# One 512-column product for two token streams in a feed-forward's up projection

## The chip, the cores and the metric

The kernel runs on one core of a Trainium2 chip. The metric is the device time of one execution in microseconds (us), the median over several runs. The core's engines are named as in the profile: PE (TensorE, matmuls), PEld (TensorE's weight loads, which overlap PE), DVE (VectorE), ACT (ScalarE), POOL (GpSimd) and SP (SyncE, which here issues the large loads).

## The reference, cut to what matters

Two small transformer models run one behind the other on 256 tokens x of width 1024. In the first model's first layer a second stream of 256 context tokens, ctx, goes through the same layer with the same weights and its own modulation, so its feed-forward takes both streams; D_FF is 2816.

```python
def modulate(h, shift, scale):
    return h * (1 + scale) + shift

def conv_ffn(h, w_up, conv_w, conv_b, w_down):
    a = h @ w_up
    a = lax.conv_general_dilated(a, conv_w, window_strides=(1,), padding=((CONV_W // 2, CONV_W // 2),),
                                 dimension_numbers=('NWC', 'WIO', 'NWC'),
                                 feature_group_count=a.shape[-1]) + conv_b
    gate, val = jnp.split(a, 2, axis=-1)
    return (jax.nn.silu(gate) * val) @ w_down

# first_block, layer i
x = x + g2 * conv_ffn(modulate(rms_norm(x, norm2_g[i]), sh2, sc2),
                      w_up[i], conv_w[i], conv_b[i], w_down[i])
if not last:
    ...
    ctx = ctx + cg2 * conv_ffn(modulate(rms_norm(ctx, norm2_g[i]), csh2, csc2),
                               w_up[i], conv_w[i], conv_b[i], w_down[i])
```

## The kernel before, in words

All is float32, and each operand of a large product is split into a high part and a low rest (wh and wl of the weights, hH and hL of the normed and modulated tokens h, gH and gL of the gated values). A product is then the sum of three matmuls, high by high (L285), high by low (L286) and low by high (L289), written once in `mms`: for each half of the inner tiles k, and in it for each output bank b, the first two kinds alternate over k, and the third follows for both banks. The weights are the stationary operand (a 128x128 tile), the tokens the moving one.

The first feed-forward, `ffn(0)` with T = 512, has 22 chunks `up` (128 gate and 128 value columns each, two PSUM banks of a tile S, of which there are two) in six groups of 4, 4, 4, 4, 3 and 3, and behind each group its `down` products, 8 tiles of 128 outputs with 512 tokens as moving columns (acc). Behind the first up of a group stands the down of the group before. Between them, as filler, are the products of a modulation (L410, weights wm loaded at L366). An up works through stream 0 (x, h in the tiles hH and hL of pool `hp`) and then through stream 1 (ctx, h in the tiles hcH and hcL of the pool of 8 KB buffers, x8), 256 moving columns each: 2 streams x 2 banks x 8 k x 3 matmuls = 96. Then ACT and DVE evacuate S with the convolution (L988, L991, L993), silu (L1021), product (L1024) and split (L1028, L1029).

Weights come as two halves w by DMA from SP (L224), are cast to wh by ACT (L238) in pieces of 384, 384 and 256 columns, and DVE subtracts to get wl (L240). Of the pairs wh, wl two stand in a pool of their own, wp; in the plan of loads every third pair takes two buffers of x8 (`wtile`). In the first feed-forward these are the pairs of up chunks 2, 6, 10, 14, 18 and 21, and of the two pairs of a down (outputs 0 to 3, outputs 4 to 7) the first, in the first four groups.

The norm in front of it, `h_split` and `h_tile`, makes h tile by tile: DVE scales (ht, L529), ACT adds the shift and rounds (L539), DVE takes the rest (L540); for some tiles of stream 0 ACT and POOL do that (L535 to L537).

PE and SP run in a written order: a planner (`Line`) interleaves the pieces of work, and each `yield` of `mms` tells it the time of a half, reckoned from columns. ACT, DVE and POOL are put in order by an automatic scheduler, which works with its own estimates of when things are ready.

Of the kernel before, what the change touches and what calls it, by code (L numbers as in the profile page):

```python
# [12 lines left out]
F32R = mybir.dt.float32r  # L13
# [6 lines left out]
P = 128  # L20
D = 1024
NT = 256
KD = D // P
# [3 lines left out]
CH = 2048  # L27
# [5 lines left out]
class Line:  # L33
# [4 lines left out]
    def __init__(self):  # L38
        self.now, self.pend, self.live = 0.0, [], {}
# [40 lines left out]
def spread(main, fill):  # L80

    out, done = [], 0
    for i, u in enumerate(main):
        out.append(u)
        want = len(fill) * (i + 1) // len(main)
        out += fill[done:want]
        done = want
    return out + fill[done:]

# [7 lines left out]
WHOLE = ()  # L99
# [6 lines left out]
class Stack:  # L106
# [406 lines left out]
            nc.tensor.matmul(ps, lhsT=self.ones, rhs=sq, start=ft == 0, stop=ft == KD - 1)  # L513
        return {"ps": ps}

    def h_room(self, s, whole=False):
        if whole:
            t = self.hp.tile([P, CH], F32, tag="hH", name="h") if s == 0 else self.x8("hc")
            self.h[s] = (t.rearrange("p (k t) -> p k t", k=KD),)
        elif s == 0:  # L520
            self.h[s] = tuple(self.hp.tile([P, KD, NT], F32R, tag=t, name=t) for t in ("hH", "hL"))
        else:
            self.h[s] = tuple(self.x8(t, F32R).rearrange("p (k t) -> p k t", k=KD) for t in ("hcH", "hcL"))
# [18 lines left out]
    def h_split(self, i, j, g, r, s, pre=None, pool=(), wait=0):  # L542


        A = self.mod_scale(i, j + 1, g, s)
        B = self.mods(i, j)
        self.h_room(s, (i, j) == (1, 0) and "win1" in WHOLE)
        for ft in range(KD):
            if pre is not None:
                pre(ft)  # L550
            self.h_tile(ft, A[:, ft:ft + 1], B[:, ft, s:s + 1], r, s, ft in pool)
            if wait and ft < KD - 1:
                yield 0, wait
# [152 lines left out]
    def block1(self, l, after):  # L706
# [233 lines left out]
        seq += heavy[:n]  # L940
        seq += need("c00", "c01", *(f"c{c}{s}" for c in (1, 2) for s in streams))
        seq += spread(bs(range(4)), spread(heavy[n:], fill[0]))
        seq += need(*(f"c{c}{s}" for c in (3, 4, 5) for s in streams), "c31", "c51")
        bnames = [f"b{p}{s}1" for p in range(4) for s in streams]
        cc = cs_()
        if l == 1:
            seq += [lambda: self.go(self.ctx2_norm(), "cx")]
        w0 = wouts(0, slice(0, T))
        seq += cc[:2] + need(*bnames) + spread(cc[2:], spread(w0, fill[1]))
        seq += need(*(f"g{s}" for s in streams))  # L950
        seq += need("c_0011", "c_1011")
        for a, b in MOVES[l]:
            seq.insert((a + b) % len(seq), seq.pop(a % len(seq)))
        if l == 1:
            seq = seq[:12] + spread(seq[12:], self.more_units((1, 12, 20)))
# [40 lines left out]
    def ffn(self, i, T, streams, after):  # L996


        nc, key = self.nc, f"sm{i}"
        post = i >= 2  # L1000
        groups = FF_GROUPS[T]
        starts = [sum(groups[:g]) for g in range(len(groups))]
        nst = {q: {} for q in streams}
        y = self.x8("y").rearrange("p (k t) -> p k t", k=KD) if post else None
        gt = {}
        cols = 512 if T == 512 else 256

        def up(g, j):
            a = j - starts[g]
            if a == 0:  # L1010
                gt[g] = tuple(self.gp.tile([P, groups[g], T], F32R, tag=t, name=t) for t in ("gH", "gL"))
            wh, wl = self.weights(f"wup{i}", j, k=KD)
            ps = self.psum("S", [P, 2, 512])
            for q in streams:
                hH, hL = self.h[q]
                yield from self.mms([ps[:, b, 256 * q:256 * q + 256] for b in range(2)], range(KD),
                         lambda b, k: (wh[:, k, P * b:P * b + P], wl[:, k, P * b:P * b + P]),
                         lambda b, k: (hH[:, k], hL[:, k]))
            c = self.pt.tile([P, 2, 512], F32, tag="pt", name="cgv")
            self.conv(c[:, 0, :T], ps[:, 0, :T], key, j)  # L1020
            nc.scalar.activation(c[:, 0, :T], c[:, 0, :T], AF.Silu)  # L1021
            if i < 2:
                self.conv(c[:, 1, :T], ps[:, 1, :T], key, KF + j)
                nc.vector.tensor_tensor(c[:, 1, :T], c[:, 0, :T], c[:, 1, :T], ALU.mult)  # L1024
            else:
                nc.vector.tensor_tensor(c[:, 1, :T], c[:, 0, :T], ps[:, 1, :T], ALU.mult)
            gH, gL = gt[g]
            nc.scalar.copy(gH[:, a], c[:, 1, :T])  # L1028
            (nc.vector if T == 512 else nc.gpsimd).tensor_tensor(gL[:, a], c[:, 1, :T], gH[:, a].bitcast(F32), ALU.subtract)  # L1029
            if j == KF - 1:  # L1030
                self.lnexp()

        def down(g, ft, c):
            gk = groups[g]
            cc, f4 = divmod(ft, cols // P)
            wh, wl = self.weights(f"wdn{i}", g, cc, k=gk)
            gH, gL = gt[g]
            fs = slice(P * f4, P * f4 + P)
            acc = self.psum("acc", [P, 512])
            yield from self.mms([acc[:, c]], range(gk), lambda b, k: (wh[:, k, fs], wl[:, k, fs]),  # L1040
                     lambda b, k: (gH[:, k, c], gL[:, k, c]))
            last = g == len(groups) - 1
            if not post:
                self.residual(i, 5, acc, ft, [q for q in streams if c.start <= 256 * q < c.stop])
                if last:
                    self.sumsq(nst[c.start // 256], self.xs[c.start // 256][:, ft], ft == KD - 1)
            else:
                if g == 0:
                    nc.scalar.copy(y[:, ft], acc[:, :256])
                else:  # L1050
                    nc.vector.tensor_tensor(y[:, ft], y[:, ft], acc[:, :256], ALU.add)
                if last:
                    self.post_sums(nst[0], y[:, ft], ft, i == 3)

        main = []
        for kind, g, j in self.ffn_order(T):
            if kind == "up":
                main.append(lambda g=g, j=j: self.go(up(g, j)))
            elif g < len(groups) - 1:
                main += [lambda g=g, ft=ft: self.go(down(g, ft, slice(0, T))) for ft in range(KD)]  # L1060
        for u in spread(main, self.fill_f(i)):
            u()
        if i == 0:
            self.prep1(1)
        if post:
            nst[0] = self.post_start(i, 5, self.sm(key, "post2"))
        for q in streams:
            for ft in range(KD):
                self.go(down(len(groups) - 1, ft, slice(256 * q, 256 * q + 256)))
                if i == 2:  # L1070
                    self.early_loads(ft)
            after(q, nst[q], y)
# [553 lines left out]
```

## Time and profile before

| | us |
|---|---|
| median of 3 runs | 1751.69 |
| lowest, highest | 1749.96, 1760.24 |
| the profiled execution's own time | 1754.48 |
| its span, first to last instruction | 1752.7 |

The profiled execution is 2.79 us above the median, and 1.8 us of its time lie outside the span. Its mean granted TensorE clock is 0.967 of full speed. The first feed-forward takes the stretch from about 312 to 716 us. A row with an operation and a number ("PE S L289 x8") gives what was written (S) and the line; the profile cuts a matmul's busy time so that in the chain of waits each piece lasts from one start to the next, while a mean in the groups counts the overlap of pipelined matmuls twice.

### The profile page before, as it was taken

Reading aid. Unit: us, or ns where it says so; the run is one execution under the profiler, and the core shown is the slowest. Engines: PE = TensorE matmul, PEld = TensorE weight load, DVE = VectorE, ACT = ScalarE, POOL = GpSimd, SP = SyncE. Lnnn points to the kernel's source line nnn. Section 1 sums busy time; section 2 is a strip of 40 time slices with the busy share of each in tenths; the row PEclk is TensorE's granted clock in tenths of the full one; section 3 lists DMA queues with packets and bytes.
Section 4 is the critical chain, followed back from the end, with each engine's and each line's share of the span. In section 5 each row is a group of like instructions: output and inputs, shape, how many; then the busy total and the mean of one; then the engine's idle time right before and its main releaser. Section 6 shows DMA issues by size and latency. Waiting matters only on the chain.

```text
span 1752.7 us, 32334 instructions
## 1 busy us (share of the span) xinstructions
PE 1599.5 (91%) x12604; PEld 1419.1 (81%) x12604; DVE 1188.5 (68%) x2877; ACT 879.1 (50%) x2147; POOL 136.7 (8%) x162
## 2 busy tenths in 40 slices
PE   6999797999999999889888998988979999779997
PEld 5877457989898989788468998976869999479996
DVE  5765886755555545777788777785776567876665
ACT  6344654523242324455546656563556555656563
POOL 1000001000000000010000101000141012330110
PEclk9999998999999999999899999999989999889999
DMA  8344330444545454334334544565554546435552
GB/s 326 107 145 145 125 125 32 146 182 177 219 143 217 168 205 176 131 119 154 133 109 151 195 167 139 175 220 208 197 180 164 196 155 226 174 118 196 170 176 88
DMA packets 67402, 288.36 MB, mean 165 GB/s; under 512 B 7728, under 2 KB 9008, under 8 KB 54960
## 3 DMA queue, kind: packets, MB, share of 16 engines
q1 hardware_dynamic: 65664, 283.91, 46.0%
q10 hardware_dynamic: 1584, 2.38, 0.4%
q8 instruction: 99, 1.62, 0.4%
q14 instruction: 55, 0.45, 0.1%
HBM read 285.21 MB, written 1.05 MB: 163 GB/s over the span
## 4 chain that ended last, share of the span: by engine, by line
PE 61%; DVE 18%; DMA 10%; ACT 7%; issue 3%; POOL 1%; SPq 0%; ACTq 0%; DVEq 0%; POOLq 0%
PE S L285 9%; PE S L286 9%; PE S L289 9%; PE acc L285 8%; PE acc L286 8%; PE acc L289 8%; DVE wl L240 6%; DMA w<-in_wup_dram 5%; PE acc L410 3%; ACT wh L238 2%; DMA w<-in_wdn_dram 2%; DVE ht L529 1%; PE tr L671 1%; DMA wm<-in_wmod_dram 1%; DVE mx L661 1%
## 5 line engine op out<-in xcount | busy, mean ns | idle before, releaser
L240 DVE TENSOR_TENSOR wl<-w,wh 128x384 fp32r<-128x384 f32 (+2 forms) x1010 | 489.1, 523 | 218.5 <-ACT wh L238 190.7
L238 ACT CAST wh<-w 128x384 fp32r<-128x384 f32 (+2 forms) x1010 | 421.3, 475 | 329.4 <-DMA w<-in_wup_dram 94.9
L285 PE MATMUL S<-hH,wh 128*128 128x256 f32 x1408 | 351.3, 287 | 31.0 <-ACT hH L539 17.4
L286 PE MATMUL S<-hL,wh 128*128 128x256 f32 x1408 | 349.2, 285 | 4.7 <-POOL hL L537 4.0
L285 PEld LDWEIGHTS S<-hH,wh 128*128 128x128 f32 x1408 | 271.6, 193 | 36.9 <-ACT hH L539 18.1
L286 PEld LDWEIGHTS S<-hL,wh 128*128 128x128 f32 x1408 | 271.5, 193 | 7.1 <-POOL hL L537 5.0
L285 PE MATMUL acc<-gH,wh 128*128 128x256 f32 (+1 forms) x728 | 209.0, 311 | 9.2 <-DVE xc L980 4.8
L286 PE MATMUL acc<-gL,wh 128*128 128x256 f32 (+1 forms) x728 | 205.3, 306 | 0.0
L289 PE MATMUL S<-hH,wl 128*128 128x256 f32 x1408 | 198.4, 284 | 0.0
L289 PEld LDWEIGHTS S<-hH,wl 128*128 128x128 f32 x1408 | 182.6, 193 | 0.0
L285 PEld LDWEIGHTS acc<-gH,wh 128*128 128x128 f32 x728 | 138.9, 191 | 23.6 <-issue 7.0
L289 PE MATMUL acc<-gH,wl 128*128 128x256 f32 (+1 forms) x728 | 145.7, 306 | 0.0
L286 PEld LDWEIGHTS acc<-gL,wh 128*128 128x128 f32 x728 | 138.9, 191 | 5.5
L991 DVE SCALAR_TENSOR_TENSOR cgv<-S,sm,cgv 128x255 f32<-128x255 f32 (+1 forms) x132 | 74.8, 567 | 67.6 <-ACT cgv L988 67.1
L289 PEld LDWEIGHTS acc<-gH,wl 128*128 128x128 f32 x728 | 110.2, 191 | 6.5
L988 ACT ACTIVATE cgv<-S,sm 128x256 f32<-128x256 f32 (+1 forms) x132 | 82.7, 628 | 47.3 <-PE S L289 47.3
L285 PE MATMUL acc<-wh,hH 128*128 128x256 f32 x344 | 91.2, 296 | 10.4 <-ACT hH L539 8.2
L1029 POOL TENSOR_TENSOR gL<-cgv,gH 128x256 fp32r<-128x256 f32 x66 | 52.2, 791 | 579.5 <-ACT gH L1028 558.7
L980 DVE SCALAR_TENSOR_TENSOR x<-acc,mod,x 128x256 f32<-128x256 f32 x104 | 50.0, 482 | 57.7 <-PE acc L289 57.3
L286 PE MATMUL acc<-wl,hH 128*128 128x256 f32 x344 | 88.1, 287 | 0.0
L286 PE MATMUL S<-hcL,wh 128*128 128x256 f32 x352 | 86.5, 284 | 0.3 <-DVE hcL L540 0.3
L285 PE MATMUL S<-hcH,wh 128*128 128x256 f32 x352 | 86.4, 280 | 0.0
(268 smaller groups left out, 2837.4 us busy)
## 6 DMA issues: line engine op xcount, KB each, us to landing
wm<-in_wmod_dram SPq DMA_DIRECT2D x72, 1024.0 KB, 7.6
w<-in_wup_dram SPq DMA_DIRECT2D x140, 512.0 KB, 3.9
w<-in_wdn_dram SPq DMA_DIRECT2D x56, 512.0 KB, 4.1
mw<-in_wmod_dram SPq DMA_DIRECT2D x48, 512.0 KB, 4.7
w<-in_wup_dram SPq DMA_DIRECT2D x18, 1024.0 KB, 7.5
w<-in_win_dram SPq DMA_DIRECT2D x32, 512.0 KB, 4.0
w<-in_wout_dram SPq DMA_DIRECT2D x16, 512.0 KB, 4.7
w<-in_wqkv_dram SPq DMA_DIRECT2D x16, 512.0 KB, 3.9
```

The source lines that it names most:

```text
L238: self.nc.scalar.copy(h[:, c:d], w[:, c - a:d - a])
L240: self.nc.vector.tensor_tensor(l[:, c:d], w[:, c - a:d - a], h[:, c:d].bitcast(F32), ALU.subtract)
L285: mm(o, lhsT=s[0], rhs=m[0], start=k == ks[0], stop=False)
L286: mm(o, lhsT=s[0], rhs=m[1], start=False, stop=False)
L289: mm(o, lhsT=S(b, k)[1], rhs=M(b, k)[0], start=False, stop=end and k == ks[-1])
L410: nc.tensor.matmul(acc[32 * u:32 * u + 32], lhsT=self.cpad[:, k], rhs=w[:, 256 * u:256 * u + 256], start=k == ks[0], stop=k == ks[-1])
L529: nc.vector.scalar_tensor_tensor(t, self.xs[s][:, ft], A, r, ALU.mult, ALU.mult)
L661: nc.vector.tensor_reduce(mx, S[:, :, :nk], AX.X, ALU.max)
L980: self.nc.vector.scalar_tensor_tensor(x, acc[:, c], self.mods(i, j)[:, ft, s:s + 1], x, ALU.mult, ALU.add)
L988: nc.scalar.activation(out, ps, AF.Identity, scale=cw[:, n + f:n + f + 1], bias=cb[:, f:f + 1])
L991: nc.vector.scalar_tensor_tensor(o[:, :, 1:256], x[:, :, 0:255], cw[:, f:f + 1], o[:, :, 1:256], ALU.mult, ALU.add)
L1029: (nc.vector if T == 512 else nc.gpsimd).tensor_tensor(gL[:, a], c[:, 1, :T], gH[:, a].bitcast(F32), ALU.subtract)
```

## The change

`h_room` gets a third layout for the norm in front of the first feed-forward: two hp tiles h hold the high parts of both streams, inner tiles 0 to 3 in one and 4 to 7 in the other, with the 512 tokens of both streams side by side for each inner tile; two x8 tiles hc hold the low parts in the same way. `Halves` indexes such a pair of tiles. The norm of either stream writes its 256 columns. In `up`, chunk 0 still takes the streams one after the other; every later chunk takes both in one call of `mms`, with 512 moving columns, which fill a bank.

```diff
--- before.py
+++ after.py
@@ -86,6 +86,17 @@
         out += fill[done:want]
         done = want
     return out + fill[done:]
+
+
+class Halves:
+
+
+    def __init__(self, tiles):
+        self.t = tiles
+
+    def __getitem__(self, at):
+        p, k, *rest = at
+        return self.t[k // 4][(p, k % 4, *rest)]
 
 
 
@@ -513,8 +524,16 @@
             nc.tensor.matmul(ps, lhsT=self.ones, rhs=sq, start=ft == 0, stop=ft == KD - 1)
         return {"ps": ps}
 
-    def h_room(self, s, whole=False):
-        if whole:
+    def h_room(self, s, whole=False, joint=False):
+        if joint:
+            if s == 0:
+                both = ([self.hp.tile([P, CH], F32R, tag=t, name="h") for t in ("hH", "hL")],
+                        [self.x8("hc", F32R) for _ in range(2)])
+                both = [[t.rearrange("p (k c) -> p k c", k=4) for t in ts] for ts in both]
+                self.both = [Halves(ts) for ts in both]
+                for q in range(2):
+                    self.h[q] = tuple(Halves([t[:, :, NT * q:NT * q + NT] for t in ts]) for ts in both)
+        elif whole:
             t = self.hp.tile([P, CH], F32, tag="hH", name="h") if s == 0 else self.x8("hc")
             self.h[s] = (t.rearrange("p (k t) -> p k t", k=KD),)
         elif s == 0:
@@ -544,7 +563,7 @@
 
         A = self.mod_scale(i, j + 1, g, s)
         B = self.mods(i, j)
-        self.h_room(s, (i, j) == (1, 0) and "win1" in WHOLE)
+        self.h_room(s, (i, j) == (1, 0) and "win1" in WHOLE, (i, j) == (0, 3))
         for ft in range(KD):
             if pre is not None:
                 pre(ft)
@@ -1011,9 +1030,12 @@
                 gt[g] = tuple(self.gp.tile([P, groups[g], T], F32R, tag=t, name=t) for t in ("gH", "gL"))
             wh, wl = self.weights(f"wup{i}", j, k=KD)
             ps = self.psum("S", [P, 2, 512])
-            for q in streams:
-                hH, hL = self.h[q]
-                yield from self.mms([ps[:, b, 256 * q:256 * q + 256] for b in range(2)], range(KD),
+            if j and T == 512:
+                parts = [(self.both, slice(0, T))]
+            else:
+                parts = [(self.h[q], slice(256 * q, 256 * q + 256)) for q in streams]
+            for (hH, hL), c in parts:
+                yield from self.mms([ps[:, b, c] for b in range(2)], range(KD),
                          lambda b, k: (wh[:, k, P * b:P * b + P], wl[:, k, P * b:P * b + P]),
                          lambda b, k: (hH[:, k], hL[:, k]))
             c = self.pt.tile([P, 2, 512], F32, tag="pt", name="cgv")
```

Lines of the changed file lie 11 to 22 higher: L296, L297 and L300 are the three matmuls, L249 the cast, L251 the subtraction, L1007 the first evacuation.

On PE, inside up chunk 1 of the first feed-forward, where stream 0 ends and stream 1 begins before the change:

```order
L285 MATMUL S<-hH,wh 128x256
L286 MATMUL S<-hL,wh 128x256
L289 MATMUL S<-hH,wl 128x256 x8
L285 MATMUL S<-hcH,wh 128x256
L286 MATMUL S<-hcL,wh 128x256
L285 MATMUL S<-hcH,wh 128x256
```

and at the place of the chunk's two halves of k now:

```order
L296 MATMUL S<-h,wh 128x512
L297 MATMUL S<-hc,wh 128x512
L300 MATMUL S<-h,wl 128x512 x8
L296 MATMUL S<-h,wh 128x512
L297 MATMUL S<-hc,wh 128x512
L296 MATMUL S<-h,wh 128x512
```

Two matmuls of 256 columns that shared a stationary tile are one of 512 now: 48 in place of 96 in an up, in the same order over k and banks. PE and SP keep the order of everything else.

On ACT, around the evacuation of an early up (cgv<-S is the evacuation, wh<-w a weight cast), before:

```order
L238 CAST wh<-w 128x384 x2
L238 CAST wh<-w 128x256
L988 ACTIVATE cgv<-S,sm_97 128x512
L238 CAST wh<-w 128x384 x2
L238 CAST wh<-w 128x256
L1021 ACTIVATE cgv<-cgv 128x512
L988 ACTIVATE cgv<-S,sm_97 128x512
L1028 CAST gH<-cgv 128x512
L238 CAST wh<-w 128x384 x2
L238 CAST wh<-w 128x256
L988 ACTIVATE cgv<-S,sm_97 128x512
```

and now:

```order
L249 CAST wh<-w 128x384 x2
L249 CAST wh<-w 128x256
L249 CAST wh<-w 128x384
L1007 ACTIVATE cgv<-S,sm_97 128x512
L249 CAST wh<-w 128x384
L249 CAST wh<-w 128x256
L1043 ACTIVATE cgv<-cgv 128x512
L1007 ACTIVATE cgv<-S,sm_97 128x512
L1050 CAST gH<-cgv 128x512
L249 CAST wh<-w 128x384 x2
L249 CAST wh<-w 128x256
L249 CAST wh<-w 128x384 x2
```

One piece of the next half of a weight is now cast ahead of the evacuation that it stood behind; there are about five such places in the stage.

On DVE, at the norm of stream 1 (ht is the scaled tile, hcL and hc the low part, mscale and mod_108 of the modulation), before:

```order
L529 SCALAR_TENSOR_TENSOR ht<-xc,mscale,rstd 128x256 x3
L540 SCALAR_TENSOR_TENSOR hcL<-ht,mod_108,hcH 128x256 x3
L529 SCALAR_TENSOR_TENSOR ht<-xc,mscale,rstd 128x256 x3
L540 SCALAR_TENSOR_TENSOR hcL<-ht,mod_108,hcH 128x256 x3
L529 SCALAR_TENSOR_TENSOR ht<-xc,mscale,rstd 128x256 x2
L240 TENSOR_TENSOR wl<-w,wh 128x384
L540 SCALAR_TENSOR_TENSOR hcL<-ht,mod_108,hcH 128x256 x2
L240 TENSOR_TENSOR wl<-w,wh 128x384
```

and now:

```order
L548 SCALAR_TENSOR_TENSOR ht<-xc,mscale,rstd 128x256 x4
L559 SCALAR_TENSOR_TENSOR hc<-ht,mod_108,h 128x256 x4
L548 SCALAR_TENSOR_TENSOR ht<-xc,mscale,rstd 128x256 x3
L559 SCALAR_TENSOR_TENSOR hc<-ht,mod_108,h 128x256 x3
L548 SCALAR_TENSOR_TENSOR ht<-xc,mscale,rstd 128x256
L251 TENSOR_TENSOR wl<-w,wh 128x384 x2
L559 SCALAR_TENSOR_TENSOR hc<-ht,mod_108,h 128x256
L251 TENSOR_TENSOR wl<-w,wh 128x256
```

The tiles go in runs of 4, 3 and 1 in place of 3, 3 and 2, and two weight pieces in place of one stand ahead of the last low part. DVE's order is also changed in the last group of downs, where weight pieces stand further ahead of the modulation's sums; ACT, DVE and POOL have their old order from the second layer on.

## Rows read from the trace of the kernel before

**Rows 1.** The page, busy time: engine, us busy, share of the span, instructions.

```profile
PE 1599.5 (91%) x12604; PEld 1419.1 (81%) x12604; DVE 1188.5 (68%) x2877; ACT 879.1 (50%) x2147; POOL 136.7 (8%) x162
```

**Rows 2.** The page, chain that ended last: shares by engine and line.

```profile
PE 61%; DVE 18%; DMA 10%; ACT 7%; issue 3%; POOL 1%; SPq 0%; ACTq 0%; DVEq 0%; POOLq 0%
PE S L285 9%; PE S L286 9%; PE S L289 9%; PE acc L285 8%; PE acc L286 8%; PE acc L289 8%; DVE wl L240 6%; DMA w<-in_wup_dram 5%; PE acc L410 3%; ACT wh L238 2%; DMA w<-in_wdn_dram 2%; DVE ht L529 1%; PE tr L671 1%; DMA wm<-in_wmod_dram 1%; 
```

**Rows 3.** Busy time in stretches of the first feed-forward, in us; PEclk, DMA share, GB/s.

```profile
core 0: us, PE busy (x) PEld busy (x) DVE busy (x) ACT busy (x) POOL busy (x), PEclk, DMA share, GB/s
400.00:450.00 50.00, 50.00 (x425) 48.48 (x424) 26.87 (x53) 20.63 (x43) 0.00 (x0) 1.00 0.40 145
```

**Rows 4.** Groups on PE by form, 325 to 690 us: busy us, mean ns.

```profile
L285 PE MATMUL S<-hH,wh 128*128 128x256 f32 x336 | 82.7, 284 | 0.0
L286 PE MATMUL S<-hcL,wh 128*128 128x256 f32 x336 | 82.5, 284 | 0.0
...
L285 PE MATMUL acc<-gH,wh 128*128 128x512 f32 x128 | 52.0, 406 | 0.0
```

**Rows 5.** Chain of waits, 422 to 462 us: start us, us, what.

```profile
435.23 0.96 PE S L289 x8
...
446.74 0.96 PE S L289 x8
...
453.49 0.47 PE acc L289 x2
...
460.52 0.47 PE acc L289 x2
```

**Rows 6.** The same view, 386 to 400 us.

```profile
390.12 0.45 PE acc L289 x2
...
394.19 0.45 PE acc L289 x2
```

**Rows 7.** Waits, 325 to 690 us: us in total, times, longest us.

```profile
ACT cgv L988 <- PE S L289: 31.3, 10, 3.9
ACT wh L238 <- DMA w<-in_wup_dram: 24.9, 12, 3.7
...
ACT wh L238 <- DMA w<-in_wdn_dram: 10.3, 7, 2.4
```

**Rows 8.** Timeline of DVE around one up: start us, us, instruction.

```profile
400.29 0.42 DVE L240 TENSOR_TENSOR wl<-w,wh 128x256 fp32r<-128x256 f32 x1
...
416.42 0.75 DVE L993 SCALAR_TENSOR_TENSOR cgv<-S,sm,cgv 128x510 f32<-128x510 f32 x1
```

**Rows 9.** Timeline of PE there.

```profile
412.70 1.11 PE L289 MATMUL S<-hH,wl 128*128 128x256 f32 x8
...
424.20 0.39 PE L285 MATMUL S<-hH,wh 128*128 128x256 f32 x1
```

**Rows 10.** Timeline of DVE at the second stream's norm.

```profile
315.61 1.28 DVE L529 SCALAR_TENSOR_TENSOR ht<-xc,mscale,rstd 128x256 f32<-128x256 f32 x3
...
319.17 1.28 DVE L540 SCALAR_TENSOR_TENSOR hcL<-ht,mod,hcH 128x256 fp32r<-128x256 f32 x3
320.36 0.89 DVE L529 SCALAR_TENSOR_TENSOR ht<-xc,mscale,rstd 128x256 f32<-128x256 f32 x2
...
321.62 0.89 DVE L540 SCALAR_TENSOR_TENSOR hcL<-ht,mod,hcH 128x256 fp32r<-128x256 f32 x2
```

**Rows 11.** Timeline of PE there.

```profile
319.07 0.38 PE L285 MATMUL S<-hcH,wh 128*128 128x256 f32 x1
319.71 0.39 PE L286 MATMUL S<-hcL,wh 128*128 128x256 f32 x1 [0.26 <-DVE hcL L540]
```

**Rows 12.** Chain of waits at the end of the first feed-forward.

```profile
704.71 0.59 SPq L366
705.35 9.22 DMA wm<-in_wmod_dram
714.62 1.07 PE acc L410 x16
```

## The prediction, as it was made before the changed kernel ran

> **What bounds the kernel now.** I read the page first, then the chain of waits, then the stage. TensorE is busy for 91% of the span [rows 1], and the chain that ended last is 61% PE; the six groups of three-part products (S and acc at L285, L286, L289) are 8 or 9% of it each [rows 2]. In the first feed-forward it is TensorE alone: in the stretch 400 to 450 us PE is busy for all 50.00 us at a granted clock of 1.00, while DVE works 26.87 us, ACT 20.63 us and the DMA engines 0.40 of the time [rows 3]. So inside this stage a matmul saved is time saved, as long as the weights keep coming.
>
> The stage holds six groups of 336 up matmuls with 256 columns after chunk 0, two of which are shown [rows 4]; the other four have the same count: 2016 in all = 21 chunks x 96. Their mean of 284 ns counts the overlap of neighbours, so I take prices from the starts in the chain instead. There "L289 x8" closes a half of k in one stream, four such in an up: from 435.23 to 446.74 us are four steps of 24 matmuls [rows 5], 11.51 us / 96 = **119.9 ns** for one of 256 columns.
>
> The same stage shows what one with 512 columns takes, in the downs. In a down of four inner tiles "L289 x2" closes six matmuls. From 453.49 to 460.52 us are five steps [rows 5]: 7.03 / 30 = **234.3 ns**; these read a weight pair that lies in x8. From 390.12 to 394.19 us are three steps [rows 6]: 4.07 / 18 = **226.1 ns**; that pair lies in wp. Both are under 2 x 119.9 = 239.8 ns: a matmul of half the columns costs more than half.
>
> **The change part by part.**
>
> *The merged products.* 21 chunks x 48 = 1008 pairs become 1008 single matmuls. A pair gives back 239.8 - 226.1 = 13.7 ns at the quick price and 239.8 - 234.3 = 5.5 ns at the slow one, 13.8 us or 5.5 us over all. Neither price is of this product: the moving data are h in hp and hc in x8 here, gH and gL there. I go by where the weights lie, the one thing that differs between the two down stretches: of the 21 chunks, 15 have their pair in wp and 6 (chunks 2, 6, 10, 14, 18, 21) in x8. That is 15 x 48 x 13.7 + 6 x 48 x 5.5 = 9864 + 1584 ns = **11.4 us**; both ends stay for the range. All of it lies on the path, since PE does not wait in the stage.
>
> The Trainium skill (TensorE: Matmul & The Clock Gate, Back-to-back issue gap) gives an isolated gap as columns / 2.4 GHz plus about 2.5 ns. By that a merged pair would give back only 2.5 ns, 1008 x 2.5 = 2.5 us, an estimate from the page. The rows disagree: both the 119.9 and the 226.1 ns lie some 13 ns above columns over 2.4 GHz, so the fixed part here is larger, and the measurement decides. The same section has a sustained spacing of about 131 ns at 512 columns; the 226.1 and 234.3 ns of this trace contradict it.
>
> *The weights must come faster.* The matmuls of an up shrink by some 0.5 us from 11.5 us, so the supply has 5% less time. Chunk 6's last piece of wl ends at 400.29 + 0.42 = 400.7 us [rows 8] and is first read at 412.70 us [rows 9]: 12.0 us ahead. Over the whole stage PE would gain 11.4 us on the supply if that stood still, but the cast and the subtraction mostly wait for PE to free a buffer, and DVE and ACT have half their time free [rows 3]. The waits for weight DMAs, 24.9 us in 12 and 10.3 us in 7, are at most 3.7 us long [rows 7], against 12.0 us of lead. I cost this at nothing; that cover gone, the worst row would cost 3.7 us at a place.
>
> *The order on ACT.* At about five places a cast stands ahead of an evacuation that it followed before. If its half of the weights has not landed, the evacuation waits too, and behind it silu, the split and the freeing of S. What covers it: S has two buffers, chunk 5's last reader ends at 416.42 + 0.75 = 417.2 us [rows 8], and chunk 7 first writes that buffer at 424.20 us [rows 9], 7.0 us later; the longest DMA wait of 3.7 us fits into it. So I cost this at nothing too; ACT itself stood waiting for PE ahead of ten evacuations, up to 3.9 us [rows 7].
>
> *The norm of stream 1.* PE waits once in chunk 0: after 319.07 us it stands until 319.71 us for the fourth low part [rows 11], because DVE makes three scaled tiles, three low parts, then three scaled tiles [rows 10]. In runs of four the fourth low part ends at 315.61 + 8 x 0.40 = 318.8 us, before it is wanted: 0.6 us gained. But the eighth now stands behind a run of one and two weight pieces: with steps of 0.40 (0.47 for a piece) DVE gets there at 315.61 + 15 x 0.40 + 2 x 0.47 = 322.6, and ends 0.4 us later, at 323.0 us; PE, come 0.64 us earlier, wants it at 322.0. It waits 0.97 us. Net a loss of **0.3 us**, between a gain of 0.3 (if the scheduler's pieces are short) and a loss of 0.4.
>
> *The end of the stage.* The last modulation weights are issued at 704.71 us and land at 705.35 + 9.22 = 714.57 us, for which PE waits [rows 12]. What holds that issue is DVE's subtractions, which free the buffers of the loads queued ahead on SP. They stand earlier in DVE's order now, which could save PE's idle time there of under 1 us; or the sums that they pass come late, by up to four pieces of 0.55 = 2.2 us. I take 0, and -0.9 to +2.2 for the range.
>
> *Unchanged.* Chunk 0 and the two x8 buffers for low parts cost no more than before: stream 1's two tiles took x8 buffers already. Everything behind the stage keeps its order and moves as a whole.
>
> **The sum**: -11.4 + 0.3 + 0 = -11.1 us. On the profiled execution that is 1754.5 - 11.1 = 1743.4 us; its 2.8 us above the median carry over, so against the median 1751.7 - 11.1 = **1740.6 us**, 0.6% less. About 1% (17.5 us) is what a measurement of this kernel can tell from no change, so this counts as within it.
>
> **The rivals.**
>
> 1. *All products at the slow price.* If it is the low halves in x8 that slow a 512-column matmul, every chunk pays 234.3 ns: -5.5 + 0.3 = -5.2 us, 1746.5 us. For: the slow down stretch also reads x8. Against: with 256 columns the groups that read hH in hp and hcL in x8 have the same mean of 284 ns [rows 4]. Chance 0.2.
>
> 2. *The supply or the end of the stage takes it all.* PE gains on weights until a place waits for a DMA or a cast, or the sums at the end come 2.2 us late and a wait of 3.7 us appears: -11.4 + 0.3 + 2.2 + 2 x 3.7 = -1.5, some 1750 us. Against: a lead of 12.0 us and half-idle DVE and ACT. Chance 0.1.
>
> 3. *ACT's queue makes it slower.* A cast waits for its DMA in front of an evacuation, S is not freed, and PE stops; PE's stop then delays the freeing of weight buffers and with it the next loads. It decides once the cast waits for more than the 7.0 us of slack. The nearest row is a DMA wait of 3.7 us; were each of the five places late by 7.0 + 3.7, PE would lose 5 x 3.7 = 18.5 us: -11.1 + 18.5 = +7.4, 1759 us. Against: such a wait would be three times the longest of this stage. Chance 0.06, two thirds of it past +1%, since a stopped PE passes the delay on.
>
> 4. *More than the rows show.* If the pair in S gave back more than 17.5 ns each, the gain would pass 1%: 1008 x 17.5 = 17.6 us, 1734 us. For it a 512-column matmul would need 222 ns, under any stretch read here. Chance 0.04.
>
> That the change doesn't do what it says is excluded by the order on PE, which has 48 matmuls of 512 columns per later chunk.
>
> **How the numbers follow.** The forecast has 0.6, the rivals 0.2, 0.1, 0.06 and 0.04. The forecast's own ends are -13.8 - 0.3 - 0.9 = -15.0 (1736.7 us) and, with the slow price, -5.5 + 0.4 + 2.2 = -2.9 (1748.8 us). Medians of the kernel before spread by 1.7 us downward, so the range is 1735.5 to 1750.5 us; it holds rivals 1 and 2 and leaves out 3 and 4. Faster by over 1%: rival 4, 0.04; slower by over 1%: 0.04; within 1%: 0.92.
>
> **What the profile after would show.** In the stage's chain, steps of 24 matmuls with "S L300 x8" at 5.43 us (quick) or 5.62 us (slow) in place of two of 2.88 us; six chunks of 21 at the slow price and the others at the quick one if the place of the weights decides. PE still busy all through, and the first down starting earlier by 0.5 us per chunk passed. At stream 1's norm no wait at the fourth low part and one of about 1 us at the eighth. ACT's waits for weight DMAs in front of an evacuation would be the sign of rival 3, idle PE between 330 and 690 us that of rival 2. I am wrong above all if the price of 512 columns in S is not between 226 and 234 ns.

## The result

The changed kernel is slower: 1766.04 us in the median of six runs (1763.58 to 1767.63) against 1754.03 us for the kernel before, also of six, a ratio of 1.0054 with a 95% interval of 1.0036 to 1.0072. I had forecast 1740.6 us. Its profiled execution took 1765.89 us with a span of 1764.1 us and a granted clock of 0.957.

**The stage itself did what was forecast, by two thirds.** In the stretch 400 to 450 us of the changed kernel TensorE is still busy throughout at a granted clock of 1.00, and DVE and ACT have half their time left [rows 3]:

```profile
400.00:450.00 50.00, 50.00 (x256) 39.29 (x249) 27.83 (x55) 21.39 (x46) 0.00 (x0) 1.00 0.47 168
```

The groups by form, 331 to 690 us, have 336 matmuls of 512 columns in each of three groups where there were six of 256 [rows 4]:

```profile
L297 PE MATMUL S<-hc,wh 128*128 128x512 f32 x336 | 133.2, 396 | 0.0
L296 PE MATMUL S<-h,wh 128*128 128x512 f32 x336 | 132.6, 395 | 0.0
```

In its chain of waits (start us, us, what), where "L300 x8" closes a step of 24 products:

```profile
407.66 1.85 PE S L300 x8
...
413.21 1.85 PE S L300 x8
...
418.84 1.87 PE S L300 x8
...
424.47 1.87 PE S L300 x8
```

The first step is 5.55 us, or 231.3 ns for a product; the other two belong to chunk 6, whose weights lie in x8, and take 5.63 us each, 234.6 ns. Chunks 2 and 3 repeat it in the same view, with 5.63 us (weights in x8) and 5.56 us. Two of 256 columns took 239.8 ns in a chunk with its weights in wp [rows 5]. In chunk 6 of the kernel before they took less; its four steps, in that kernel's chain of waits:

```profile
410.01 0.96 PE S L289 x8
...
421.45 0.96 PE S L289 x8
```

That is 11.44 us / 96 = 119.2 ns, or 238.3 ns for two.

The waits, 331 to 690 us (total, times, longest), name the weight loads as before, those of w_dn for longer in total (16.9 against 10.3 us) [rows 7]:

```profile
ACT wh L249 <- DMA w<-in_wup_dram: 21.9, 12, 3.2
ACT cgv L1007 <- PE S L300: 19.5, 7, 4.2
ACT wh L249 <- DMA w<-in_wdn_dram: 16.9, 8, 3.6
```

The norm of stream 1 (DVE, then TensorE) shows the low part that comes late and TensorE's wait for it [rows 10, 11]:

```profile
321.08 1.67 DVE L548 SCALAR_TENSOR_TENSOR ht<-xc,mscale,rstd 128x256 f32<-128x256 f32 x4
...
326.63 0.48 DVE L548 SCALAR_TENSOR_TENSOR ht<-xc,mscale,rstd 128x256 f32<-128x256 f32 x1
327.02 1.02 DVE L251 TENSOR_TENSOR wl<-w,wh 128x384 fp32r<-128x384 f32 x2
327.96 0.48 DVE L559 SCALAR_TENSOR_TENSOR hc<-ht,mod,h 128x256 fp32r<-128x256 f32 x1
```

```profile
328.49 0.38 PE L297 MATMUL S<-hc,wh 128*128 128x256 f32 x1 [0.41 <-DVE hc L559]
```

And the chain at the end of the stage runs through loads of w in place of the modulation weights [rows 12]:

```profile
699.11 3.55 DMA w<-in_wdn_dram
...
705.73 6.96 DMA w<-in_win_dram
...
714.68 0.34 DVE msum L427
```

**The loss lies outside the stage.** Four evacuations on ACT mark the first and the last of the first feed-forward and the first and the last of the second one. In the kernel before (timeline of ACT):

```profile
324.93 0.78 ACT L988 ACTIVATE cgv<-S,sm 128x512 f32<-128x512 f32 x1 [3.14 <-PE S L289]
...
692.67 0.76 ACT L988 ACTIVATE cgv<-S,sm 128x512 f32<-128x512 f32 x1
...
934.79 0.56 ACT L988 ACTIVATE cgv<-S,sm 128x256 f32<-128x256 f32 x1 [2.48 <-PE S L289]
...
1101.47 0.55 ACT L988 ACTIVATE cgv<-S,sm 128x256 f32<-128x256 f32 x1
```

and in the changed kernel:

```profile
330.81 0.78 ACT L1007 ACTIVATE cgv<-S,sm 128x512 f32<-128x512 f32 x1
...
691.48 0.76 ACT L1007 ACTIVATE cgv<-S,sm 128x512 f32<-128x512 f32 x1
...
936.66 0.56 ACT L1007 ACTIVATE cgv<-S,sm 128x256 f32<-128x256 f32 x1 [2.49 <-PE S L300]
...
1109.00 0.55 ACT L1007 ACTIVATE cgv<-S,sm 128x256 f32<-128x256 f32 x1
```

The first stretch fell from 367.74 to 360.67 us. But it begins 5.88 us later, and from its last evacuation to the end of the span it takes 1764.1 - 691.48 = 1072.6 us against 1752.7 - 692.67 = 1060.0 us. The second feed-forward alone went from 166.68 to 172.34 us, with the same instructions in the same order. Its row of busy time (as in [rows 3]) in the kernel before and in the changed one:

```profile
934.79:1101.47 166.68, 152.72 (x1236) 150.20 (x1237) 124.81 (x278) 99.77 (x246) 18.07 (x21) 0.98 0.50 173
```

```profile
936.66:1109.00 172.34, 157.44 (x1244) 155.05 (x1245) 125.06 (x278) 100.38 (x247) 18.54 (x21) 0.96 0.50 169
```

TensorE is busy for 4.7 us longer with the same work, at a granted clock of 0.96 in place of 0.98, and idle for 0.9 us longer. So in this pair most of the loss shows as work at a lower clock; run 5 shows a loss without that.

The page shows a difference there that no line of the diff is about. Its rows on DMA (queue, packets, MB, share; then loads, KB each, median us from issue to landing) for the kernel before, where q8 is a queue that fetches instructions (TensorE's, as run 9 shows):

```profile
q8 instruction: 99, 1.62, 0.4%
...
w<-in_wup_dram SPq DMA_DIRECT2D x140, 512.0 KB, 3.9
...
w<-in_win_dram SPq DMA_DIRECT2D x32, 512.0 KB, 4.0
...
w<-in_wqkv_dram SPq DMA_DIRECT2D x16, 512.0 KB, 3.9
```

and for the changed kernel:

```profile
q8 instruction: 91, 1.49, 0.3%
...
w<-in_wup_dram SPq DMA_DIRECT2D x140, 512.0 KB, 4.2
...
w<-in_win_dram SPq DMA_DIRECT2D x32, 512.0 KB, 4.3
...
w<-in_wqkv_dram SPq DMA_DIRECT2D x16, 512.0 KB, 4.1
```

The weight loads are slower, also those of w_in, half of which are issued ahead of the stage. Over the 348 transfers that SP issues outside the first feed-forward (before 300 us or after 730 us; all loads but four; the same 348 in every run, taken from the DMA records and averaged from issue to landing) it is 5.36 us in the mean against 5.18 us. Slower loads can cost time where TensorE waits for them. The chain of waits does not show that they set this loss, though: in the second feed-forward loads of w_up are 28% of it in the kernel before and 22% in the changed one.

### The profile page after: what moved, and what is told of

Same layout as the page of the kernel before. It is cut to its first block, busy times and chain, and to the rows that moved or that the text cites. A ratio compares the mean times of both kernels' runs of the same rounds, so it can differ in the third digit from the quotient of the medians.

```text
span 1764.1 us, 30314 instructions
## 1 busy us (share of the span) xinstructions
PE 1608.5 (91%) x11596; PEld 1378.3 (78%) x11596; DVE 1191.2 (68%) x2877; ACT 880.6 (50%) x2147; POOL 137.7 (8%) x162
## 3 DMA queue, kind: packets, MB, share of 16 engines
q8 instruction: 91, 1.49, 0.3%
## 4 chain that ended last, share of the span: by engine, by line
PE 60%; DVE 18%; DMA 11%; ACT 7%; issue 3%; POOL 1%; SPq 0%; ACTq 0%; DVEq 0%; POOLq 0%
PE acc L296 9%; PE S L296 8%; PE S L297 8%; PE acc L297 8%; PE S L300 8%; PE acc L300 8%; DVE wl L251 6%; DMA w<-in_wup_dram 5%; PE acc L421 3%; ACT wh L249 2%; DMA w<-in_wdn_dram 2%; PE tr L690 1%; DVE ht L548 1%; DVE mx L680 1%; DMA w<-in_wout_dram 1%
## 5 line engine op out<-in xcount | busy, mean ns | idle before, releaser
L251 DVE TENSOR_TENSOR wl<-w,wh 128x384 fp32r<-128x384 f32 (+2 forms) x1010 | 490.0, 525 | 231.2 <-ACT wh L249 190.5
L249 ACT CAST wh<-w 128x384 fp32r<-128x384 f32 (+2 forms) x1010 | 422.5, 477 | 340.5 <-DMA w<-in_wup_dram 104.6
L296 PE MATMUL S<-hH,wh 128*128 128x256 f32 x1056 | 265.9, 289 | 33.8 <-ACT hH L558 17.4
L297 PE MATMUL S<-hL,wh 128*128 128x256 f32 x1056 | 264.5, 287 | 4.3 <-POOL hL L556 3.6
L296 PEld LDWEIGHTS S<-hH,wh 128*128 128x128 f32 x1056 | 205.7, 195 | 38.2 <-ACT hH L558 18.1
L296 PE MATMUL acc<-gH,wh 128*128 128x256 f32 (+1 forms) x728 | 210.0, 312 | 9.2 <-DVE xc L999 4.8
L297 PEld LDWEIGHTS S<-hL,wh 128*128 128x128 f32 x1056 | 205.4, 195 | 6.2 <-POOL hL L556 4.3
L297 PE MATMUL acc<-gL,wh 128*128 128x256 f32 (+1 forms) x728 | 206.3, 307 | 0.0
L296 PEld LDWEIGHTS acc<-gH,wh 128*128 128x128 f32 x728 | 139.6, 192 | 23.8 <-issue 7.8
L300 PE MATMUL S<-hH,wl 128*128 128x256 f32 x1056 | 151.1, 287 | 0.0
L300 PE MATMUL acc<-gH,wl 128*128 128x256 f32 (+1 forms) x728 | 146.3, 307 | 0.0
L297 PEld LDWEIGHTS acc<-gL,wh 128*128 128x128 f32 x728 | 139.8, 192 | 5.7
L297 PE MATMUL S<-hc,wh 128*128 128x512 f32 (+1 forms) x368 | 141.1, 387 | 0.4 <-DVE hc L559 0.4
L296 PE MATMUL S<-h,wh 128*128 128x512 f32 (+1 forms) x368 | 140.8, 385 | 0.2 <-ACT h L558 0.2
L300 PEld LDWEIGHTS S<-hH,wl 128*128 128x128 f32 x1056 | 139.3, 196 | 0.0
L300 PEld LDWEIGHTS acc<-gH,wl 128*128 128x128 f32 x728 | 110.7, 192 | 6.5
L296 PE MATMUL acc<-wh,hH 128*128 128x256 f32 x344 | 92.0, 298 | 9.8 <-ACT hH L558 8.0
L1007 ACT ACTIVATE cgv<-S,sm 128x256 f32<-128x256 f32 (+1 forms) x132 | 83.0, 630 | 32.7 <-PE S L300 32.6
L300 PE MATMUL S<-h,wl 128*128 128x512 f32 (+1 forms) x368 | 89.2, 384 | 0.0
```

The lines of the kernel that those rows point to most:

```text
L249: self.nc.scalar.copy(h[:, c:d], w[:, c - a:d - a])
L251: self.nc.vector.tensor_tensor(l[:, c:d], w[:, c - a:d - a], h[:, c:d].bitcast(F32), ALU.subtract)
L296: mm(o, lhsT=s[0], rhs=m[0], start=k == ks[0], stop=False)
L297: mm(o, lhsT=s[0], rhs=m[1], start=False, stop=False)
L300: mm(o, lhsT=S(b, k)[1], rhs=M(b, k)[0], start=False, stop=end and k == ks[-1])
L1007: nc.scalar.activation(out, ps, AF.Identity, scale=cw[:, n + f:n + f + 1], bias=cb[:, f:f + 1])
```

## The experiments

Each run gave a profile. The last table collects from each the row q8, the mean of the 348 loads, and the two stretches between evacuations.

**1. Both kernels again, unchanged.** For the kernel before:

> The kernel before, unchanged, for a second profile. In the profile of the changed kernel the first feed-forward itself is 7.8 us shorter, but the stretch ahead of it is 5.5 us longer and the one behind it 13 us longer, although the order there is the same; the time at half clock in the records is 153 us against 116 us. If what lies outside the stage differs from execution to execution whatever the program (theory R), this second profile reaches the feed-forward and the end up to 6 and 13 us later or earlier than the first one, and the ratio is 1.000 with an interval of some 0.3%. If the change itself does it (theories D and C below), this profile agrees with the first within 3 us at each milestone.

For the changed kernel:

> The changed kernel once more. Theory R: the ratio lies somewhere else than 1.0054, below 1.000 if the stage's 7.8 us is all that is real. Theories D (order and buffers) and C (the granted clock behind the stage): 1.004 to 1.007 again, with about 150 us at half clock in the profile.

Measured 0.9999 (0.9981 to 1.0017) and 1.0048 (1.0032 to 1.0063), with second feed-forwards of 164.16 and 174.03 us and loads of 5.13 and 5.42 us. Theory R falls as an account of the loss: it is not the luck of an execution. Single stretches do vary with the same program, by 2.5 us in the two profiles of the kernel before: 327.46 us here against 324.93 us ahead of the stage, 164.16 against 166.68 us in the second feed-forward. There the changed kernel's TensorE is busy 4.1 us longer and idle 5.8 us longer in this pair, so the shares of lower clock and of waiting change from pair to pair.

**2. The new tiles without the 512 columns.**

```diff
-            if j and T == 512:
+            if False:
                 parts = [(self.both, slice(0, T))]
```

> The joint tiles of the changed kernel, but every up chunk takes the streams one after the other with 256 columns, as before. Theory D: the new tiles rotate the x8 buffers and change the automatic order on ACT and DVE, which costs what was lost outside the stage; then this run has that loss without the gain, 1.008 to 1.011. Theory C: with the stage as long as before, the stretch behind it is as before too: 1.000 within 0.3%.

Measured 0.998 (0.9966 to 0.9994), second feed-forward 164.05 us, loads 5.19 us. Of theory D the tiles fall: the joint tiles and their buffers cost nothing. The other half, the changed order on ACT and DVE, is hardly in this run, since without the 512 columns ACT casts ahead of an evacuation at one place in place of 16; runs 4 and 8 have that order in full and are without the loss.

**3. A shorter stage with the old tiles.** High by low is left out in two chunks.

```diff
-                         lambda b, k: (hH[:, k], hL[:, k]))
+                         lambda b, k: (hH[:, k], hL[:, k]), less=T == 512 and j in (1, 2))
```

> The kernel before with 64 matmuls of the product high by low left out in chunks 1 and 2 of the first feed-forward (those chunks lack that part of the sum), so that the stage is 64 x 119.9 ns = 7.7 us shorter and all behind it comes earlier, with the old tiles. Theory C (what lies behind a shorter stage is granted less clock): slower than before although it has less work, 1.002 to 1.006. Theory D: faster by the 7.7 us, 0.9956. Theory R: 0.9956 as well.

Measured 0.9963 (0.9946 to 0.998), 1748.05 us, which is 7.6 us less than the kernel before in this comparison; the stretch itself is 6.5 us shorter (361.27 us). The gain comes through to the end, so theory C falls too: a shorter stage in itself costs nothing behind it.

What was left was the 512-column products themselves (theory E), or that TensorE's program has become 2016 instructions shorter (1008 matmuls and a weight load with each), which could act on what comes ahead of them as well (theory M).

**4. The old length, with all 512-column products.** The tail changes nothing ahead of it.

```diff
         self.ffn(3, 256, (0,), after3)
+        ps = self.psum("tr", [P, 512])[:, :16]
+        for _ in range(504):
+            self.nc.tensor.matmul(ps, lhsT=self.ones, rhs=self.ones[:, :16], start=True, stop=True)
```

> The changed kernel with 504 float32 matmuls of 16 columns behind the last product of the program, which bring TensorE's program back to the size that it had before (1.63 MB, 1.50 MB in the changed kernel); no result uses them. Theory M (the shorter program itself is loaded to, or fetched from, other places, and the weight loads get slower by it): the loads have their old times (mean of the w_up loads 4.75 us, against 5.0 in the changed kernel), the stretch from the first to the last evacuation of the second feed-forward is 164 to 167 us as before and not 172 to 174, and the first evacuation of the first feed-forward comes at 325 to 328.8 us. Theory E (executing 512-column products leaves something behind): 172 to 174 us and 5.0 us as in the changed kernel. The time over all says nothing, because of the tail.

```profile
q8 instruction: 99, 1.62, 0.3%
...
w<-in_wup_dram SPq DMA_DIRECT2D x140, 512.0 KB, 3.9
```

```profile
928.12 0.56 ACT L1007 ACTIVATE cgv<-S,sm 128x256 f32<-128x256 f32 x1 [2.50 <-PE S L300]
...
1093.72 0.55 ACT L1007 ACTIVATE cgv<-S,sm 128x256 f32<-128x256 f32 x1
```

The page and the second feed-forward's first and last evacuation: 99 fetches as before, loads at 3.9 us, and a stretch of 165.60 us. The first feed-forward keeps its gain with 360.67 us. Its last evacuation came 9.1 us ahead of that of the kernel before in the last feed-forward (1689.39 against 1698.51 us).

**5. The new length, with no 512-column product in S.**

```diff
-                         lambda b, k: (hH[:, k], hL[:, k]))
+                         lambda b, k: (hH[:, k], hL[:, k]), less=T == 512 and j > 0 or i == 3 and j < 10)
...
-                     lambda b, k: (gH[:, k, c], gL[:, k, c]))
+                     lambda b, k: (gH[:, k, c], gL[:, k, c]), less=T == 512)
```

> The kernel before with 1008 matmuls of the product high by low left out (in chunks 1 to 21 and the downs of the first feed-forward and in ten chunks of the last one, whose sums lack that part): TensorE's program is as short as that of the changed kernel (1.50 MB), with no 512-column product in S and the old tiles. Theory M: the second feed-forward's stretch takes 172 to 174 us and the w_up loads 5.0 us. Theory E: 164 to 167 us and 4.75 us.

```profile
q8 instruction: 91, 1.49, 0.4%
...
w<-in_wup_dram SPq DMA_DIRECT2D x140, 512.0 KB, 4.4
```

```profile
835.54 0.56 ACT L989 ACTIVATE cgv<-S,sm 128x256 f32<-128x256 f32 x1 [2.49 <-PE S L290]
...
1006.48 0.55 ACT L989 ACTIVATE cgv<-S,sm 128x256 f32<-128x256 f32 x1
```

91 fetches, loads at 4.4 us, a stretch of 170.94 us, a little under the forecast of 172: the loss is there without the change. And here it is all waiting:

```profile
835.54:1006.48 170.94, 152.13 (x1237) 149.87 (x1238) 126.17 (x278) 100.51 (x246) 17.73 (x21) 0.99 0.50 169
```

TensorE is busy for 152.13 us at a granted clock of 0.99, no longer than in the kernel before, and idle for 18.8 us against 14.0 us. Runs 4 and 5 together, one profile each, speak for theory M and against E: the slow loads and the longer stretch come with the shorter program, and not with the 512-column products.

**6. Half of the chunks.**

```diff
-            if j and T == 512:
+            if j > 11 and T == 512:
```

> The changed kernel with 512 columns only from chunk 12 on (10 of the 21 chunks). The first feed-forward's stretch is about half as much shorter, 3.5 us. Theory M: TensorE's program is 1.57 MB; loads and the second feed-forward lie between, or fall to one side if a certain size decides. Theory E: the second feed-forward is half as much longer, 168 to 170 us; the time over all 1.002 to 1.004.

Measured 0.9965 (0.994 to 0.999), first stretch 363.79 us, loads 5.04 us: half of the gain and none of the loss.

**7. Twenty and sixteen chunks, and the place of the inputs.**

```diff
-            if j and T == 512:
+            if j >= 2 and T == 512:
```

> 512 columns from chunk 2 on (20 of 21 chunks; TensorE's program 1.505 MB, 6 KB longer than in the changed kernel). Theory M with a smooth effect of the length, or theory E: as the changed kernel, 1.004 to 1.005, loads at 5.35 to 5.40 us. Theory M where single lengths decide: either 1.005 or 0.996.

The same with `j >= 6`:

> 512 columns from chunk 6 on (16 of 21 chunks; 1.529 MB). The first feed-forward is some 5.4 us shorter than before. If a length between 1.505 and 1.566 MB is the border, this run shows on which side 1.529 MB lies: loads of 5.05 to 5.2 us and a time of 0.996, or loads of 5.35 us and a time of 1.003. Theory E (the executed 512-column products): second feed-forward 170 to 172 us, 1.003.

An input that nothing reads, ahead of the others:

```diff
+    packed = {"pad": np.zeros((63, 512), np.float32), **packed}
     for name, v in packed.items():
```

> The changed kernel with one more input of 129,024 bytes that nothing reads, ahead of the others: as many bytes as TensorE's program has become shorter. If what counts is where the weights lie in memory, behind the programs (theory M1), loads outside the first feed-forward take 5.15 us in the mean as before and not 5.36 to 5.41, the second feed-forward's stretch is 164 to 167 us, and the time is 0.995 of the kernel before. If it is the program's own length or place (theory M2), all stays as in the changed kernel: 5.36 to 5.41 us, 172 to 174 us, 1.005.

Measured 1.0057 (1.0039 to 1.0075), 1.0041 (1.002 to 1.0063) and 1.0041 (1.0013 to 1.0068), loads 5.39, 5.34 and 5.37 us. Even sixteen chunks are on the slow side, and adding to the inputs what the program lost does not help (theory M1 falls in that form; M2, the program's own length or place, is left).

**8. No-ops behind the 512-column products.** One behind each:

```diff
+        def mm(o, **kw):
+            self.nc.tensor.matmul(o, **kw)
+            if len(outs) == 2 and o.shape[-1] == 512:
+                for _ in range(1):
+                    self.nc.tensor.nop("pad")
-        mm = self.nc.tensor.matmul
```

> The changed kernel with one no-op in TensorE's queue behind each of the 1008 products of 512 columns: its program is 1.563 MB long in place of 1.499 MB, close to the 1.566 MB of the run with 512 columns from chunk 12 on. Theory M2 (length or place of TensorE's own program sets how fast the loads run), with a border between 1.529 and 1.566 MB: loads outside the first feed-forward back to 5.05 to 5.2 us, the second feed-forward's stretch 164 to 167 us, and, if the no-ops are hidden behind the products, 360.7 us for the first one and a time of 0.995. Theory E (the 512-column products themselves): as the changed kernel, 1.005, or slower by what the no-ops cost.

Two behind each (`range(2)`):

> The same with two no-ops behind each product: 1.6276 MB, the length of the kernel before within 64 bytes. Theory M2: 5.15 us for the loads, 164 to 167 us, 0.995 to 0.996. Theory E: 1.005 or more. If single lengths decide and not a border, this run and the one with one no-op may differ, and this one has to be as the kernel before.

Measured 0.9961 (0.9943 to 0.998) and **0.9919 (0.9901 to 0.9937)**. The second, 1745.68 us where the kernel before took 1758.85 us in the same comparison, beats both kernels. In its profile, the stretch 400 to 500 us, the rows on DMA, and the four evacuations:

```profile
400.00:500.00 100.00, 100.00 (x551) 76.87 (x550) 53.26 (x104) 35.26 (x73) 0.00 (x0) 1.00 0.50 183
```

```profile
q8 instruction: 99, 1.62, 0.4%
...
w<-in_wup_dram SPq DMA_DIRECT2D x140, 512.0 KB, 4.1
```

```profile
324.53 0.78 ACT L1011 ACTIVATE cgv<-S,sm 128x512 f32<-128x512 f32 x1
...
685.20 0.76 ACT L1011 ACTIVATE cgv<-S,sm 128x512 f32<-128x512 f32 x1
...
927.84 0.56 ACT L1011 ACTIVATE cgv<-S,sm 128x256 f32<-128x256 f32 x1 [2.47 <-PE S L285]
...
1094.74 0.55 ACT L1011 ACTIVATE cgv<-S,sm 128x256 f32<-128x256 f32 x1
```

TensorE is as busy as without the no-ops and the stage as short, 360.67 us: they are hidden. The second feed-forward is back at 166.90 us.

**9. Is it the length, whose length, and is there a border?** Three behind each:

> Three no-ops behind each product: TensorE's program is 1.692 MB, longer than in any kernel so far. If a border between 1.531 and 1.563 MB decides, the loads stay at 5.15 us and the time at 0.992 to 0.996. If single lengths decide, either side is possible. If the no-ops were what helps, by pacing TensorE and not by their length, this is at least as fast as two of them.

One behind every other product:

> One no-op behind every other product: 1.531 MB, the length of the run with 512 columns from chunk 6 on (1.529 MB), but with all 21 chunks at 512 columns. Theory M2: slow loads, 5.35 us, and 1.003 to 1.005, as the changed kernel. If no-ops in themselves help, about half of what one behind each product gives: 1.000.

And 2016 no-ops on SyncE behind the last work:

```diff
         self.ffn(3, 256, (0,), after3)
+        for _ in range(2016):
+            self.nc.sync.nop("pad")
```

> The changed kernel with 2016 no-ops at the end of SyncE's queue: the programs together are as long as before, TensorE's stays at 1.499 MB. If TensorE's own program is what counts: loads of 5.36 to 5.41 us and 172 to 174 us in the second feed-forward. If the sum of the programs counts, by the place of what lies behind them: 5.15 us and 164 to 167 us. The time over all says nothing, because of the tail.

Measured 0.9987 (0.9958 to 1.0015) for three and 1.0017 (0.9989 to 1.0044) for one behind every other, with loads of 5.20 and 5.43 us; so 504 no-ops that leave the program at 93 fetches give no quick loads, which speaks against pacing. The loads are on the forecast sides, the times are not: three no-ops missed 0.992 to 0.996, one behind every other missed 1.003 to 1.005, and neither time is clear of the kernel before. Three are one too many for the stage, which takes 362.57 us; that is 1.9 us of the miss. With the no-ops on SyncE the loads stay at 5.35 us and the second feed-forward at 174.24 us. Its page also shows whose fetches the rows count:

```profile
q8 instruction: 91, 1.49, 0.3%
q14 instruction: 71, 0.57, 0.1%
```

q8 stays at 91, so it is TensorE's own program; it is q14 that grew, from 0.45 to 0.57 MB.

All runs, by the length fetched (time ratios above; the tails' times say nothing):

| run | q8: fetches, MB | 348 loads, mean us | first, second feed-forward, us |
|---|---|---|---|
| changed | 91, 1.49 | 5.36 | 360.67, 172.34 |
| changed again | 91, 1.49 | 5.42 | 360.86, 174.03 |
| products left out (5) | 91, 1.49 | 5.36 | 273.68, 170.94 |
| idle input | 91, 1.49 | 5.37 | 360.67, 174.13 |
| no-ops on SyncE | 91, 1.49 | 5.35 | 360.67, 174.24 |
| from chunk 2 | 92, 1.51 | 5.39 | 361.02, 171.84 |
| from chunk 6 | 93, 1.52 | 5.34 | 362.17, 169.48 |
| a no-op behind every other | 93, 1.52 | 5.43 | 360.67, 174.68 |
| from chunk 12 | 95, 1.56 | 5.04 | 363.79, 166.86 |
| one no-op | 95, 1.56 | 5.14 | 360.66, 167.11 |
| before | 99, 1.62 | 5.18 | 367.74, 166.68 |
| before again | 99, 1.62 | 5.13 | 367.75, 164.16 |
| new tiles, 256 columns | 99, 1.62 | 5.19 | 366.57, 164.05 |
| two chunks shortened | 99, 1.62 | 5.21 | 361.27, 163.51 |
| tail | 99, 1.62 | 5.17 | 360.67, 165.60 |
| two no-ops | 99, 1.62 | 5.20 | 360.67, 166.90 |
| three no-ops | 103, 1.69 | 5.20 | 362.57, 166.00 |

Sorted by length the loads fall into two groups with nothing between: eight runs up to 93 fetches at 5.34 to 5.43 us, nine from 95 fetches on at 5.04 to 5.21 us. The second feed-forward follows: 169.5 to 174.7 us, and 163.5 to 167.1 us. So does all that lies behind the stage, from the last evacuation of the first feed-forward to the end of the span: 1069.5 to 1075.1 us in the six runs of the first group that change nothing there, 1056.1 to 1062.7 us in the eight of the second, 13.9 us apart in the mean.

The stretch ahead of the stage doesn't follow. It goes with the granted clock, over both groups: 322.49 us at 0.97 (run 5), 324.93 at 0.96 (before), 325.39 at 0.96 (idle input), 330.39 at 0.94 (one no-op), 330.81 at 0.94 (changed), 335.02 at 0.93 (three no-ops).

## Why the prediction was wrong, point by point

**The merged products**: mechanism right, size off. I had 11.4 us from prices of 226.1 and 234.3 ns. That six chunks with weights in x8 pay the slow price and fifteen the quick one held, but the quick price in S is 231.3 ns, not the 226.1 ns of a down, and a pair in x8 took 238.3 ns and not 239.8: 15 x 48 x (239.8 - 231.3) + 6 x 48 x (238.3 - 234.6) = 7.2 us. The stretch shows 7.1 us. The quick down is another stream (gH and gL as moving data), and a price from it is a bound, as I had said, and no middle.

An isolated gap by the Trainium skill (TensorE: Matmul & The Clock Gate, Back-to-back issue gap) would be 512 / 2.4 GHz plus about 2.5 ns, 216 ns. The trace disagrees with 231.3 ns, and the gain of 7.1 us is nearly three times the 2.5 us that I had estimated from the page.

**The weights must come faster, and the order on ACT**: both cost nothing, as forecast, though the second was described too small. In the trace ACT casts one or two pieces ahead of an evacuation at 16 places, 26 pieces in all, and not one piece at about five. TensorE stays busy, the waits for weight DMAs in the stage are at most 3.6 us long, and rivals 2 and 3 show no sign.

**The norm**: 0.3 us forecast; DVE's scaled tiles begin 321.08 - 315.61 = 5.47 us later and the first evacuation 5.88 us, so 0.41 us are lost there, as described. The wait at the eighth tile is 1.06 us (0.97 forecast), first for ACT's high part and then for DVE's low one; the wait at the fourth is gone.

**The end of the stage**: 0 taken; the offset to the kernel before goes from -1.2 us at the last evacuation to -2.1 us at the first residual of stream 1's last group (724.26 against 726.32 us in DVE's timeline), a gain of 0.9 us, the end of my range.

**The step that failed** is "Everything behind the stage keeps its order and moves as a whole". It keeps its order, and the stretch from the last evacuation to the end takes 12.6 us longer (18.2 us in the repeated pair of profiles). I had looked at queues, buffers and order, and not at the removal of 2016 instructions as an effect in itself. In its place the runs showed this: with TensorE's program at 91 to 93 fetches a load takes 0.2 us more in the mean, whether or not 512-column products run in S, and the part behind the stage takes 13.9 us more; with 95 fetches or more neither is so. The second feed-forward loses 5.7 us of it (172.34 against 166.68), 9.9 in the repeated pair. None of my rivals had this, so neither the range nor the 0.04 for a loss of more than 1% had a case for it. With one no-op or two the change is faster than the kernel before, as I took it to be; with three the time tells nothing.

**The range**: 1736.7 us less the spread of 1.7 us is 1735.0 us and not 1735.5; nothing hangs on it. And I took 1% for what a measurement can tell, where the interval here is 0.18% to each side, so that the loss of 0.54% is clear of the noise.

**What stays open.** How the length of TensorE's program, or the place of what lies behind it, reaches the weight loads is not shown; it is neither the place of the inputs, as far as one idle input tells, nor the length of SyncE's program. That the slower loads in their turn cost the 13.9 us is argued from the two going together in every run, and the chain of waits doesn't show it: in the repeated pair the share of w_up loads in the second feed-forward is 18.5% and 18.9%. Why the loss is now waiting and now a lower clock is open too. Why two no-ops give 0.9919 and one 0.9961, with loads and stages alike, is open in part: the stage's 7.1 us are 0.4%, and the runs with two had a granted clock of 0.965 to 0.968, those of the kernel before beside them 0.958 to 0.966. Time and clock go together in one and the same program: among 19 runs of the kernel before in the last comparison the shortest took 1746.64 us at 0.970 and the longest 1764.47 us at 0.960. So 0.9919 has luck with the clock in it, as far as the runs tell, and 0.996 is nearer to what the change is worth.

## What to carry to other kernels

A change that removes instructions from the longest program changes the kernel outside its own place; when a time moves the wrong way, compare the durations of what was not touched, and read the granted clock of each stretch beside them, since here the stretch ahead of the change went with the clock and not with the change. The test was cheap: add no-ops on the engine that has time for them until the program has its old length, and judge the change then. And a price from a like instruction in another stream of the same stage was 5 ns off, which was a third of the gain that I forecast.

## What the runs showed of the hardware

Weight loads of unchanged size and order took 5.34 to 5.43 us in the mean with 91 to 93 fetches of TensorE's program and 5.04 to 5.21 us with 95 to 103, whatever the length came from: left-out products, merged ones, no-ops or a tail. No-ops on TensorE's queue, up to two behind each 512-column product, cost nothing (360.67 us with and without); a third cost 1.9 us over the 1008. The part behind the stage took 1069.5 to 1075.1 and 1056.1 to 1062.7 us in the two groups. A product of 512 columns took 231.3 ns with its weights in wp and 234.6 ns with them in x8, where two of 256 columns took 239.8 and 238.3 ns. The stretch ahead of the stage took 322.49 us at a granted clock of 0.97 and 335.02 us at 0.93.
